# Moving one row of DRAM copies later, and summing half of an output projection in loaded tiles instead of with accumulating DMAs

## The chip, the cores and the metric

The kernel runs on one core of a Trainium2 chip. TensorE (PE) does the matmuls, VectorE (DVE) and ScalarE (ACT) do the elementwise work, GpSimd (POOL) issues the accumulating DMAs, and SyncE (SP) issues all other DMAs, in one in-order queue. The metric is the device time in microseconds of one execution; lower is better, and the median of several executions counts.

## The reference

A decoder trunk of one layer, 1024 tokens by 2048 channels, fp32:

```
hn = rmsnorm(h, norm_gain)
proj = hn @ w_in
pool_in, pool_gate, ssm_in, ssm_gate = four blocks of 1024 columns of proj
ya = pool_mixer(pool_in, w_pool, pool_scale) * silu(pool_gate)
yb = ssm_mixer(ssm_in, ...) * silu(ssm_gate)
h = h + concatenate([ya, yb]) @ w_out
h = h + (p @ w_ple) * sigmoid(h @ w_ple_gate)
return rmsnorm(h, final_gain)
```

## The kernel before, in words

Activations are kept transposed (channels on the 128 partitions, tokens along the row, 512 tokens to a half). Each fp32 operand is split in a rounded high part and a low rest, and a product is three matmuls (high by high, high by low, low by high). The split of a weight tile is a ScalarE cast (L204 in the output projection) and a VectorE subtraction (L103).

**Steps.** The program is one list of steps, written out in order by `emit(s)`. A step issues weight loads and the stores that have become due (`store(o, i, n)` is issued n+1 steps later, by SP), splits the weights of steps up to two ahead, calls the functions hung on it as `pre`, issues its matmuls, and calls those hung on it as `post`, which evacuate PSUM. So the position of a function in the step list sets where its instructions stand in each engine's in-order queue.

**Units.** The output projection is 8 units of 14 steps of 12 matmuls each: a unit makes 256 channels by two halves of 512 tokens of 512 columns of `w_out`, with a Strassen-like scheme of seven products (`PRODS`) by b = 0, 1. `units[0..3]` sum over the first 1024 rows of `w_out` (n = 0: slab `("y", 0)`, made of ya), `units[4..7]` over the second 1024 (n = 1, yb), each for the four column groups cg = 0 to 3; in this text they are units 0 to 7. A unit has eight results (4 row blocks of 128 channels by 2 halves of 512 tokens, 256 KB each).

**How a result leaves.** The sum lives in DRAM: `xT_d`, 2048 channels by 1024 tokens, holds the residual. In `o_post`, ScalarE copies four of a unit's products (each by b) from PSUM to an SBUF tile `ot` (L1294), VectorE adds the others to it, and POOL adds the tile to `xT_d` with an accumulating DMA (L1288). That is done for all 8 units. The gate is computed from this sum, and its results (for the first 1536 channels) are later accumulated by POOL to a second copy of it, `z_d`. Three plain copies by SP, DRAM to DRAM, of 512 rows (2 MB) each, fill `z_d`:

```
    for cg in range(3):

        steps[units[5 + cg][1] + 8]["pre"].append(lambda cg=cg: sp.dma_start(
            out=z_d[cg * HT:(cg + 1) * HT], in_=xT_d[cg * HT:(cg + 1) * HT]))
```

They stand at step 8 of units 5, 6 and 7.

**The slab of the gate.** Units 8 to 13 (gate, `w_ple_gate`) multiply with the slab of the finished h. While units 6 and 7 still run, the first half of that slab is made: `sums_load` (L378) reads rows of `xT_d` into `cq` at unit 6's steps 1, 5, 9 and 13, `sums_make` forms four sums of them 5 steps later, which go to `cm_d` by plain stores (L186, three steps later); `comb_load` (L397) reads the 28 tiles `cb` of the slab, from `xT_d` or `cm_d`, into a pool of 32 slots as they become free in unit 7, and `comb_split` (L402 on ScalarE) casts them, from step 4 of unit 7 on. ScalarE is in order: what is behind a cast whose load has not landed waits, the next weight cast (L204) too.

**The last columns' weights.** `wl_d` in DRAM is filled from the last 512 columns of `w_ple_gate` by 16 plain copies DRAM to DRAM of 256 KB (L1527), one every two steps from step `i_wl` on; it is read only at the end of the kernel. `vu` (L857) and `vb` (L869) are the loads of the state-space branch's small products (L882), `raw` (L194) those of `w_in`.

Of the kernel before, what the change touches and what calls it, by code (L numbers as in the profile page):

```python
# [12 lines left out]
ALU = mybir.AluOpType  # L13
# [5 lines left out]
HT = 512  # L19
# [20 lines left out]
def hybrid_trunk(ctx: ExitStack, tc: tile.TileContext, x, p, norm_gain, w_in, w_pool, pool_scale,  # L40
# [3 lines left out]
    sp = nc.sync  # L44
    dve = nc.vector
# [6 lines left out]
    out = out[0]  # L52
# [19 lines left out]
    xT_d = dr.tile([D, L], F32, name="xT_d")  # L72
# [11 lines left out]
    z_d = dr.tile([3 * HT, L], F32, name="z_d")  # L84
# [5 lines left out]
    def st(dt=F32, shape=(P, HT), name="st"):  # L90
        return st_p.tile(list(shape), dt, tag="st", name=name)
# [10 lines left out]
    def tt(eng, o, a, b, op):  # L102
        eng.tensor_tensor(out=o, in0=a, in1=b, op=op)  # L103
# [46 lines left out]
    steps = []  # L150
# [20 lines left out]
    banks = {}  # L171
# [5 lines left out]
    def store(o, i, n=1):  # L177

        late.append([n, o, i])
# [190 lines left out]
    def pair(src, i, h):  # L370
        return src[i * P:(i + 1) * P, h * HT:(h + 1) * HT]
# [159 lines left out]
    for h in range(2):  # L531
        for c0 in range(0, KD, 4):
# [7 lines left out]
            for kk, mb in chs:  # L540
                k = c0 + kk
                first.setdefault((h, k // 2), len(steps))
                last = k + 2 == KD
# [4 lines left out]
    for (h, j), at in first.items():  # L548
        at = max(1, at - X1)
# [5 lines left out]
    for h in range(2):  # L555
        at = first[h, 7] - 4
# [556 lines left out]
    def in_block(mb, halves=(0, 1)):  # L1113
        block(in_cols(mb), ALLK, halves, hn_key, ("pi", mb), v_post(mb))
        if 1 in halves:
            steps[-1]["post"].append(lambda: bg.append(pool_win(mb // 2, mb % 2)))
# [10 lines left out]
    in_block(6)  # L1127
    in_block(7)
    i_g = len(steps)
    i_wl = i_g - 120  # L1130
    in_block(4)
    pool_mm(3)
    in_block(5)
# [140 lines left out]
    for i in range(8):  # L1274
        at = i_g + 5 * i
# [7 lines left out]
    def o_post(n, cg):  # L1283
        def post(prod, b):
            name = ("o", n, cg)

            def add(c, h, t):
                pool.dma_start(out=pair(xT_d, 4 * cg + 2 * c + b, h), in_=t, accum_op=ALU.add)  # L1288

            if prod in ("11", "s2", "s3", "s4"):  # L1290
                k, c, h = {"11": ("a", 0, 0), "s2": ("a", 0, 1), "s3": ("e", 1, 1),
                           "s4": ("a", 1, 0)}[prod]
                t = ot[c, h, b] = st(name="ot")
                act.copy(out=t, in_=banks[name, k, b])  # L1294
                if prod == "s4":
                    add(c, h, ot.pop((c, h, b)))
                return
            k, c, h = {"12": ("f", 0, 0), "s1": ("a", 1, 1), "22": ("e", 0, 1)}[prod]
            t = ot.pop((c, h, b))
            tt(dve, t, banks[name, k, b], t, ALU.add)  # L1300
            add(c, h, t)
        return post

    units = []
# [8 lines left out]
    zt = {}  # L1313

    def z_load(src, mb, h, key):
        zt[key, mb, h] = st(name="z" + key)
        sp.dma_start(out=zt[key, mb, h], in_=pair(src, mb, h))
# [39 lines left out]
                                ps_d if key == "s" else e_d, mb, h, key))  # L1357
    for cg in range(3):

        steps[units[5 + cg][1] + 8]["pre"].append(lambda cg=cg: sp.dma_start(  # L1360
            out=z_d[cg * HT:(cg + 1) * HT], in_=xT_d[cg * HT:(cg + 1) * HT]))
    i_d = len(steps)
    for i, (u, s0) in enumerate(units):
        at = (units[i - 1] if i else gu[3])[1] + 2
# [6 lines left out]
    for j, s0, d in ((0, gu[1][1], 6), (1, i_c, 7), (3, units[6][1] - 3, 4), (4, units[8][1], 6)):  # L1371
        for kp in range(4):
            at = s0 + 4 + d * kp
# [3 lines left out]
    for j, s0 in ((0, gu[3][1]), (1, units[3][1]), (2, None), (3, units[7][1]),  # L1377
                  (4, units[10][1])):
        for i, prod in enumerate(PRODS):
            for kp in range(4):  # L1380
                n = 4 * i + kp
                if s0 is not None:
                    at = s0 + 2 * i + 4 + kp // 2
                elif n < 12:
                    at = i_last0 + 5 + n
                else:
                    at = i_last1 + 2 + (n - 12)
# [135 lines left out]
    for k in range(KD):  # L1523
        at = s_l + 4 + 2 * (k // 4) + k % 4 // 2
# [3 lines left out]
            out=wl_d[k * P:(k + 1) * P], in_=w_ple_gate[:, k, 3 * GW:]))  # L1528
    steps[s_l - 8]["pre"].append(fg_load)
    for tb in range(NB):  # L1530
        for g in range(4):
            at = s_l + 2 + g // 2 if tb == 0 else i_t[0] + g - 1 if tb == 1 else i_t[tb - 2] + g
            steps[at]["pre"].append(lambda tb=tb, g=g: h_load(tb, g))
            at = max(at + 3, i_t[tb - 1] + g) if tb else s_l + 6 + g
            steps[at]["pre"].append(lambda tb=tb, g=g: h_split(tb, g))
            if tb == 0:
                at = i_t[0] + {3: 1, 0: 2, 1: 3, 2: 4}[g]
            else:
                at = i_t[tb] + g + (tb == 1)
# [80 lines left out]
```

## Time and profile before

| what | value |
|---|---|
| median of 3 executions | 1695.04 us (1694.57 to 1695.71) |
| the profiled execution | 1694.17 us |
| its span | 1692.4 us |
| PE busy | 1650.8 us (98%) |
| DVE, ACT, POOL busy | 1116.8, 716.7, 160.2 us |
| DMA moved | 340.61 MB, mean 201 GB/s |

The span runs from the first to the last instruction that the profiler recorded; the device time of the same execution is 1.77 us longer. Busy shares are averages over the whole span. Where a change is made in one stage, the rows of that stage are to be read: its window, what ended TensorE's idle time there, and what the DMA engines did in it.

### The profile page before, as it was taken

Reading aid. Unit: us, or ns where it says so; the run is one execution under the profiler, and the core shown is the slowest. Engines: PE = TensorE matmul, PEld = TensorE weight load, DVE = VectorE, ACT = ScalarE, POOL = GpSimd, SP = SyncE. Lnnn points to the kernel's source line nnn. Section 1 sums busy time; section 2 is a strip of 40 time slices with the busy share of each in tenths; the row PEclk is TensorE's granted clock in tenths of the full one; section 3 lists DMA queues with packets and bytes.
Section 4 is the critical chain, followed back from the end, with each engine's and each line's share of the span. In section 5 each row is a group of like instructions: output and inputs, shape, how many; then the busy total and the mean of one; then the engine's idle time right before and its main releaser. Section 6 shows DMA issues by size and latency. Waiting matters only on the chain.

```text
span 1692.4 us, 22974 instructions
## 1 busy us (share of the span) xinstructions
PE 1650.8 (98%) x7622; PEld 1364.9 (81%) x7622; DVE 1116.8 (66%) x2148; ACT 716.7 (42%) x1511; POOL 160.2 (9%) x267
## 2 busy tenths in 40 slices
PE   8999999999999999999999999999999899999997
PEld 7888887887888888888778877888887688788886
DVE  6763699458797765555745778557646666877754
ACT  6652255352213552334643345335432533634553
POOL 0067000000000210000000000211111100011100
PEclk9999999999999999999999999999999899999999
DMA  8862444672233772687884576869679966989995
GB/s 264 253 189 74 117 133 138 197 207 89 75 113 100 217 213 73 186 233 227 275 300 149 189 271 205 225 156 274 147 183 267 318 232 225 340 221 264 273 281 158
DMA packets 334408, 340.61 MB, mean 201 GB/s; under 512 B 56281, under 2 KB 225266, under 8 KB 333298
## 3 DMA queue, kind: packets, MB, share of 16 engines
q1 hardware_dynamic: 321618, 316.07, 58.2%
q0 software_dynamic: 12672, 23.07, 8.6%
q8 instruction: 60, 0.98, 0.2%
q14 instruction: 58, 0.48, 0.1%
HBM read 226.34 MB, written 123.21 MB: 207 GB/s over the span
## 4 chain that ended last, share of the span: by engine, by line
PE 49%; DMA 4%; DVE 3%; issue 2%; ACT 1%; SPq 0%; ACTq 0%; POOLq 0%; POOL 0%; DVEq 0%
PE mm L236 24%; PE aux L236 10%; PE mm L258 8%; PE mm L248 5%; DMA cb<-cm_d 1%; DVE cb L103 1%; PE bk L1459 1%; DVE w L103 1%; DMA cb<-ya_d 1%; DMA wq<-in_w_ple_gate_dram 1%; DMA e_d<-et 1%; DMA cb<-xT_d 0%; DMA wl<-wl_d 0%; DVE zs L103 0%; DMA zs<-ps_d 0%
## 5 line engine op out<-in xcount | busy, mean ns | idle before, releaser
L258 PE MATMUL mm<-hn,w 128*128 128x512 f32 x3072 | 721.8, 392 | 1.7 <-DVE w L103 1.2
L258 PEld LDWEIGHTS mm<-hn,w 128*128 128x128 f32 x3072 | 571.7, 188 | 119.7 <-DVE w L103 1.6
L236 PE MATMUL mm<-cb,w 128*128 128x512 f32 x2160 | 500.9, 391 | 8.1 <-ACT w L204 3.2
L236 PEld LDWEIGHTS mm<-cb,w 128*128 128x128 f32 x2160 | 405.5, 188 | 97.9 <-DVE w L103 5.2
L214 ACT CAST w<-raw 128x256 fp32r<-128x256 f32 x324 | 128.1, 407 | 279.2 <-PE mm L258 224.7
L103 DVE TENSOR_TENSOR w<-raw,w 128x256 fp32r<-128x256 f32 (+1 forms) x328 | 141.3, 442 | 120.0 <-ACT w L214 111.8
L103 DVE TENSOR_TENSOR w<-wq,w 128x512 fp32r<-128x512 f32 x216 | 148.6, 688 | 104.0 <-ACT w L204 103.6
L236 PE MATMUL aux<-cb,w 128*128 128x512 f32 x864 | 205.9, 393 | 6.7 <-ACT w L204 6.5
L236 PEld LDWEIGHTS aux<-cb,w 128*128 128x128 f32 x864 | 163.3, 190 | 43.5 <-ACT w L204 8.3
L204 ACT CAST w<-wq 128x512 fp32r<-128x512 f32 x216 | 133.6, 620 | 138.5 <-PE mm L236 55.8
L1288 POOL DMA_DIRECT2D xT_d<-ot x64 | 55.4, 866 | 669.5 <-DVE ot L103 636.0
L103 DVE TENSOR_TENSOR cb<-cb 128x512 fp32r<-128x512 f32 x140 | 91.8, 687 | 32.8 <-ACT cb L402 26.5
L402 ACT CAST cb<-cb 128x512 fp32r<-128x512 f32 x140 | 82.1, 621 | 39.6 <-DMA cb<-xT_d 14.3
L248 PE MATMUL mm<-wl,h 128*128 128x512 f32 (+1 forms) x432 | 96.5, 374 | 0.0
L248 PEld LDWEIGHTS mm<-wl,h 128*128 128x128 f32 x432 | 72.9, 189 | 11.9
L103 POOL TENSOR_TENSOR ytm<-yt,mask 128x512 f32<-128x512 f32 x16 | 20.1, 1255 | 446.8 <-DMA yl<-L_d 316.6
L1294 ACT COPY ot<-mm 128x512 f32<-128x512 f32 x48 | 28.2, 588 | 75.7 <-PE mm L236 75.7
L892 DVE COPY V<-aux 64x128 f32<-64x128 f32 x64 | 24.5, 382 | 29.8 <-ACT V L894 29.6
L103 DVE TENSOR_TENSOR wq<-wq 128x1024 f32<-128x1024 f32 x36 | 43.9, 1219 | 0.0
L500 ACT ACTIVATE gs<-mm 128x512 f32<-128x512 f32 x32 | 18.9, 599 | 58.1 <-DVE mm L103 58.0
L1325 POOL DMA_DIRECT2D z_d<-zs x24 | 20.7, 863 | 216.1 <-DVE zs L103 216.1
L894 ACT COPY V<-aux 64x128 f32<-64x128 f32 x64 | 24.4, 381 | 31.1 <-DVE V L892 22.4
(213 smaller groups left out, 1557.3 us busy)
## 6 DMA issues: line engine op xcount, KB each, us to landing
raw<-in_w_in_dram SPq DMA_DIRECT2D x136, 256.0 KB, 3.0
cb<-cm_d SPq DMA_DIRECT2D x80, 256.0 KB, 5.2
wq<-in_w_out_dram SPq DMA_DIRECT2D x16, 1024.0 KB, 9.2
xT_d<-ot POOLq DMA_DIRECT2D x64, 256.0 KB, 6.5
cm_d<-cq SPq DMA_DIRECT2D x48, 256.0 KB, 4.1
wq<-in_w_ple_gate_dram SPq DMA_DIRECT2D x12, 1024.0 KB, 9.0
xT_d<-xt SPq DMA_DIRECT2D x32, 256.0 KB, 3.9
wq<-in_w_glu_dram SPq DMA_DIRECT2D x16, 512.0 KB, 7.3
```

The costliest lines, as they stand in the source:

```text
L103: eng.tensor_tensor(out=o, in0=a, in1=b, op=op)
L204: act.copy(out=w[0], in_=src)
L214: act.copy(out=w[:, 0], in_=raw)
L236: pe.matmul(out=banks[key], lhsT=w[wi][:, kp], rhs=a[:, ai], start=bool(new) and n == 0, stop=n == 11, skip_group_check=True)
L248: pe.matmul(out=banks[key][:, part], lhsT=a[:, ai, cols], rhs=b[:, part], start=start and j == 0, stop=stop and j == 2)
L258: pe.matmul(out=banks[key], lhsT=w[:, wi, i], rhs=a[:, ai], start=start and i == 0 and j == 0, stop=stop and i == 1 and j == 2)
L402: act.copy(out=sl[:, 0], in_=f(sl[:, 1]))
L892: dve.tensor_copy(out=o.rearrange("p k c -> p c k"), in_=i)
L894: act.copy(out=o.rearrange("p k c -> p c k"), in_=i)
L1288: pool.dma_start(out=pair(xT_d, 4 * cg + 2 * c + b, h), in_=t, accum_op=ALU.add)
L1294: act.copy(out=t, in_=banks[name, k, b])
L1325: pool.dma_start(out=pair(z_d, mb, h), in_=t, accum_op=ALU.add)
```

## The change

Two edits. First, `i_wl` is 28 steps later, and so all 16 copies to `wl_d`. Second, in the units of n = 1 with cg < 3 (units 4, 5 and 6), eight tiles `zs` are loaded from `xT_d` three steps ahead of their first use (24 loads by SP), VectorE adds every product to the loaded tile, and the finished tile is stored twice by SP, to `xT_d` and to `z_d` (48 stores). In those units the ScalarE copies and the accumulating DMAs are gone, and the three copies `z_d<-xT_d` too. Unit 7 (cg = 3) leaves as before.

```diff
-    i_wl = i_g - 120
+    i_wl = i_g - 92
...
             def add(c, h, t):
                 pool.dma_start(out=pair(xT_d, 4 * cg + 2 * c + b, h), in_=t, accum_op=ALU.add)
 
+            if n and cg < 3:
+                k, c, h, last = {
+                    "11": ("a", 0, 0, 0), "12": ("f", 0, 0, 1), "s2": ("a", 0, 1, 0),
+                    "s3": ("e", 1, 1, 0), "s1": ("a", 1, 1, 1), "s4": ("a", 1, 0, 1),
+                    "22": ("e", 0, 1, 1)}[prod]
+                mb = 4 * cg + 2 * c + b
+                t = zt["s", mb, h]
+                tt(dve, t, banks[name, k, b], t, ALU.add)
+                if last:
+                    del zt["s", mb, h]
+                    store(pair(xT_d, mb, h), t)
+                    store(pair(z_d, mb, h), t, 2)
+                return
...
     for cg in range(3):
 
-        steps[units[5 + cg][1] + 8]["pre"].append(lambda cg=cg: sp.dma_start(
-            out=z_d[cg * HT:(cg + 1) * HT], in_=xT_d[cg * HT:(cg + 1) * HT]))
+        for at, c, h in ((0, 0, 0), (4, 0, 1), (6, 1, 1), (10, 1, 0)):
+            for b in range(2):
+                steps[units[4 + cg][1] + at + b - 3]["pre"].append(
+                    lambda mb=4 * cg + 2 * c + b, h=h: z_load(xT_d, mb, h, "s"))
```

**SP at the state-space products, before.** Weight copies stand between the loads of `raw`, `vb` and `vu`:

```order
L1527 DMA wl_d_94<-in_w_ple_gate_dram 128x512
L194 DMA raw_3377<-in_w_in_dram 128x4x128
L1527 DMA wl_d_94<-in_w_ple_gate_dram 128x512
L869 DMA vb_3385<-B_d_97 128x512
L857 DMA vu_3386<-u_d_84 128x4x128
L869 DMA vb_3404<-B_d_97 128x512
L857 DMA vu_3405<-u_d_84 128x4x128
L194 DMA raw_3420<-in_w_in_dram 128x4x128
L1527 DMA wl_d_94<-in_w_ple_gate_dram 128x512
```

Of the nine rows three are weight copies, one of them straight ahead of the first `vb`. **The same place after the change:**

```order
L194 DMA raw_3371<-in_w_in_dram 128x4x128
L869 DMA vb_3378<-B_d_97 128x512
L857 DMA vu_3379<-u_d_84 128x4x128
L869 DMA vb_3397<-B_d_97 128x512
L857 DMA vu_3398<-u_d_84 128x4x128
L194 DMA raw_3413<-in_w_in_dram 128x4x128
```

The weight copies are gone from there. **The place where they stand now**, behind the last `vu`, in the stretch in which the scan runs:

```order
L857 DMA vu_3839<-u_d_84 128x4x128
L869 DMA vb_3870<-B_d_97 128x512
L857 DMA vu_3871<-u_d_84 128x4x128
L194 DMA raw_3899<-in_w_in_dram 128x4x128
L1542 DMA wl_d_94<-in_w_ple_gate_dram 128x512
L194 DMA raw_3958<-in_w_in_dram 128x4x128
L1542 DMA wl_d_94<-in_w_ple_gate_dram 128x512
```

They alternate with the loads of `raw`, with no `vu` behind them.

**SP at the end of unit 6, before.** `cq` is read once the `cm_d` stores ahead of it are issued; `wq` is unit 8's weights:

```order
L378 DMA cq<-xT_d 128x512 x4
L186 DMA cm_d<-cs 128x512
L186 DMA cm_d<-cq 128x512 x3
L378 DMA cq<-xT_d 128x512 x4
L330 DMA wq<-in_w_ple_gate_dram 128x4x512 x2
L397 DMA cb<-xT_d 128x512 x2
```

No store of a result stands here, since POOL issues those. **The same place after:**

```order
L186 DMA cm_d<-cq 128x512 x3
L186 DMA z_d<-zs 128x512
L186 DMA xT_d<-zs 128x512
L378 DMA cq<-xT_d 128x512 x4
L186 DMA z_d<-zs 128x512
L186 DMA xT_d<-zs 128x512
L186 DMA z_d<-zs 128x512
L186 DMA xT_d<-zs 128x512
L186 DMA z_d<-zs 128x512
L330 DMA wq<-in_w_ple_gate_dram 128x4x512 x2
L397 DMA cb<-xT_d 128x512 x2
```

The results of unit 6 are stored here now, each to `xT_d` and to `z_d`: five of these stores came between the last `cq` loads and `wq`.

**SP in unit 7, before**, from the slab's loads to the next `wq`:

```order
L397 DMA cb<-xT_d 128x512 x6
L397 DMA cb<-cm_d 128x512 x2
L186 DMA cm_d<-cs 128x512
L186 DMA cm_d<-cq 128x512 x3
L397 DMA cb<-cm_d 128x512 x2
L1360 DMA z_d<-xT_d 32x16384
L397 DMA cb<-cm_d 128x512 x12
L397 DMA cb<-xT_d 128x512 x4
L330 DMA wq<-in_w_ple_gate_dram 128x4x512 x2
```

The copy to `z_d` stands ahead of twelve of the slab's loads. **After:**

```order
L397 DMA cb<-xT_d 128x512 x6
L397 DMA cb<-cm_d 128x512 x2
L186 DMA cm_d<-cs 128x512
L186 DMA cm_d<-cq 128x512 x3
L397 DMA cb<-cm_d 128x512 x14
L397 DMA cb<-xT_d 128x512 x4
L330 DMA wq<-in_w_ple_gate_dram 128x4x512 x2
```

The copy is gone, and nothing stands in its place.

## Rows read from the trace of the kernel before

**Rows 1.** The page: busy time of the engines over the span.

```profile
PE 1650.8 (98%) x7622; PEld 1364.9 (81%) x7622; DVE 1116.8 (66%) x2148; ACT 716.7 (42%) x1511; POOL 160.2 (9%) x267
```

**Rows 2.** Windows over units 3 to 7, then a stretch inside unit 7.

```profile
core 0: us, PE busy (x) PEld busy (x) DVE busy (x) ACT busy (x) POOL busy (x), PEclk, DMA share, GB/s
1143.35:1181.43 38.08, 38.08 (x169) 31.54 (x168) 29.38 (x44) 23.01 (x43) 6.90 (x8) 1.00 0.97 273
1181.43:1219.51 38.08, 38.08 (x169) 31.54 (x168) 22.57 (x33) 16.65 (x31) 6.91 (x8) 1.00 0.59 139
1219.51:1257.59 38.08, 38.08 (x169) 31.54 (x168) 17.83 (x24) 12.58 (x23) 6.90 (x8) 1.00 0.72 166
1257.59:1295.67 38.08, 38.08 (x169) 31.54 (x168) 23.01 (x32) 12.60 (x23) 6.90 (x8) 1.00 0.93 254
1295.67:1348.92 53.25, 43.81 (x169) 33.95 (x168) 34.13 (x51) 23.03 (x43) 6.44 (x8) 0.90 0.99 316
1344.00:1348.00 4.00, 4.00 (x10) 3.12 (x11) 3.85 (x7) 4.00 (x9) 1.75 (x2) 0.50 1.06 382
```

**Rows 3.** Timeline of TensorE, unit 7: start, length, form, idle before.

```profile
1305.67 8.04 PE L236 MATMUL mm<-cb,w 128*128 128x512 f32 x34 [1.22 <-DVE w L103]
...
1322.52 0.73 PE L236 MATMUL mm<-cb,w 128*128 128x512 f32 x2 [2.72 <-ACT w L204]
...
1343.73 5.36 PE L236 MATMUL aux<-cb,w 128*128 128x512 f32 x12 [4.69 <-ACT w L204]
```

**Rows 4.** Timeline of ScalarE, unit 7.

```profile
1313.65 0.62 ACT L402 CAST cb<-cb 128x512 fp32r<-128x512 f32 x1 [4.90 <-DMA cb<-xT_d]
...
1340.18 0.62 ACT L402 CAST cb<-cb 128x512 fp32r<-128x512 f32 x1 [8.28 <-DMA cb<-cm_d]
```

**Rows 5.** Timeline of SP's DMA issues, units 6 and 7.

```profile
1274.22 0.51 SPq L1360 DMA_DIRECT2D z_d<-xT_d  x1
...
1301.21 1.75 SPq L378 DMA_DIRECT2D cq<-xT_d  x4
...
1328.66 0.47 SPq L1360 DMA_DIRECT2D z_d<-xT_d  x1
1329.24 14.45 SPq L397 DMA_DIRECT2D cb<-cm_d  x12
...
1346.75 1.01 SPq L330 DMA_DIRECT2D wq<-in_w_ple_gate_dram  x2
```

**Rows 6.** Waits of SP's DMA issues, 1290 to 1350: total, times, longest.

```profile
SPq L397 <- DMA z_d<-xT_d: 5.0, 1, 5.0
```

**Rows 7.** DMA issues in unit 7's window: KB each, median us to landing.

```profile
cm_d<-cq SPq DMA_DIRECT2D x6, 256.0 KB, 9.2
```

**Rows 8.** The whole span's DMA queues and two kinds of issue.

```profile
q1 hardware_dynamic: 321618, 316.07, 58.2%
q0 software_dynamic: 12672, 23.07, 8.6%
...
ps_d<-zs SPq DMA_DIRECT2D x24, 256.0 KB, 3.8
...
z_d<-xT_d SPq DMA_DIRECT2D x3, 9.3
```

**Rows 9.** ScalarE's and VectorE's evacuations, units 4 to 6.

```profile
L1294 ACT COPY ot<-mm 128x512 f32<-128x512 f32 x18 | 10.6, 589 | 33.0 <-PE mm L236 33.0
L103 DVE TENSOR_TENSOR ot<-mm,ot 128x512 f32<-128x512 f32 x12 | 8.3, 690 | 11.6 <-PE mm L236 11.6
```

**Rows 10.** Waits of TensorE over the whole span, one of its lines.

```profile
PE aux L882 <- DMA vu<-u_d: 4.9, 3, 2.3
```

**Rows 11.** Timeline of SP's DMA issues around 345 us.

```profile
343.97 0.50 SPq L1527 DMA_DIRECT2D wl_d<-in_w_ple_gate_dram  x1
...
347.06 0.37 SPq L857 DMA_DIRECT2D vu<-u_d  x1
```

**Rows 12.** Window over the scan's stretch.

```profile
388.00:476.00 88.00, 88.00 (x390) 72.83 (x389) 71.77 (x222) 18.70 (x45) 0.00 (x0) 1.00 0.28 84
```

## The prediction

> **What bounds the kernel now.** I read the busy times first: TensorE works 1650.8 of 1692.4 us [rows 1]. So nothing that other engines or the DMAs do counts unless TensorE waits for it, and all idle time together is 41.6 us. The change takes no matmul away. The question is therefore which of those 41.6 us end on something that it moves.
>
> The windows by unit answer that for the second edit [rows 2]. Units 3 to 6 each take 38.08 us, with TensorE busy throughout and at its full granted clock (1.00, the 2.4 GHz level). Unit 7 has the same 169 matmuls and takes 53.25 us: 15.17 us more. Of these, 53.25 - 43.81 = 9.44 us are idle, and 43.81 - 38.08 = 5.73 us are matmuls at a lower clock: it is 0.90 over the unit, and 0.50 (the 1.2 GHz level) in the window that begins 0.3 us after the longest wait ended. What idled TensorE in unit 7 is in its timeline: 1.22 us on a VectorE weight tile, 2.72 and 4.69 us on ScalarE's weight casts [rows 3]. ScalarE itself, in order, was held ahead of those casts by slab casts whose loads had not landed: 4.90 us at 1313.65, 8.28 us before 1340.18 [rows 4]. The loads were late because the DMA engines were full: their share is 0.99 in unit 7 and 1.06 in its last stretch, against 0.59 to 0.93 in units 4 to 6 [rows 2]. Into this stretch SP issues, at 1328.66, the last of the 2 MB copies to z_d, and right behind it twelve slab loads that take 14.45 us to issue [rows 5]; one slab load's issue waited 5.0 us for that kind of copy alone, which it does not read [rows 6].
>
> For the first edit, the state-space products waited 4.9 us in three waits for vu [rows 10].
>
> **Prices.** The accumulating queue took 8.6% of the span, 145.5 us of all 16 engines, for 23.07 MB, which is 88 DMAs of 256 KB: 1.65 us each. The plain queue took 58.2%, 985 us, for 316.07 MB or 1206 times 256 KB: 0.82 us each [rows 8]. A 2 MB copy at that rate is 8 x 0.82 = 6.5 us; it lands 9.3 us after its issue [rows 8].
>
> **Units 4 to 6.** Per unit the second edit removes eight accumulates (13.2 us) and one copy (6.5): 19.7 us of DMA work. It adds eight loads and sixteen stores: 24 x 0.82 = 19.7 us. The work is equal; its place is not. Unit 4 goes from 0.59 x 38.08 = 22.5 us to 29.0, since no copy fell into it; unit 5 stays at 27.4 and unit 6 near 35.4 [rows 2]. All three stay under 38.08, so I cost this at nothing, hidden by TensorE's 38 us. VectorE gets eight more adds of 0.69 us, 5.5 us a unit, on top of 18 to 23 busy us of 38; ScalarE loses eight copies of 0.589, 4.7 us [rows 2, 9]. GpSimd's issues end with the accumulates.
>
> The new wait here is VectorE's first add for its zs load. Behind it in VectorE's queue stand the weight subtractions, for which TensorE would wait. The loads are issued three steps ahead, 3 x 2.72 = 8.2 us, and weights are split up to two steps ahead, another 5.4 us. A load would have to land more than 13.6 us after its issue before TensorE feels it; the slowest group in full unit 7 took a median of 9.2 us [rows 7]. I take nothing, and keep the loss for a rival.
>
> **Unit 7.** DMA work before: 0.99 x 53.25 = 52.7 us. What changes:
> - the copy at 1328.66: -6.5;
> - the four cq loads of 1301.21 [rows 5]. They belong to unit 6's last step, and were late by the copy of 1274.22, which delayed the stores ahead of them. With the copy gone they go back to unit 6: 4 x 0.82 = -3.3;
> - one accumulate of unit 6 that was issued at its end: -1.7;
> - five stores of unit 6's last results, which become due as unit 7 begins: +4.1;
> - the next weights that SP issued at 1346.75 [rows 5], which no step of unit 7 needs: -2.0 of their 6.5 by the unit's end.
>
> That makes 43.3 us of work to do in the 38.08 us, 5.2 too much. Of this the last two accumulates of unit 7 (3.3) can land in unit 8, since nothing reads them in unit 7. It leaves 1.9, and I leave the 1.22 us wait for VectorE too, because it ends on weight sums that the change doesn't touch: together 3.1 us of 15.2 stay, most of the slow clock goes with the waits, and about 12.2 us are gained. The bounds: at least the copy's own 6.5 us, if all the rest of the list is wrong; at most the whole 15.2.
>
> How would it be by unit 3? It holds 0.97 x 38.08 = 36.9 us of DMA work without any wait [rows 2]. So a unit can run with the DMA engines nearly full, and 43.3 less 3.3 is just beyond. That is why I take a value near the upper end.
>
> **First edit.** One copy is 0.50 us of SP's issue and 0.82 us of DMA work, 1.3 us. The vu load of 347.06 was issued 3.1 us behind such a copy [rows 11]; the three waits add up to 4.9 us, the longest 2.3 [rows 10]. If each shrinks by one copy's 1.3, 3.9 us go. Bounds: nothing, if vu waits for its own landing; 4.9, if all goes. In the new place, 388 to 476 us, TensorE is busy all 88 us and the DMA share is 0.28 [rows 12]: 16 copies of 0.82 us are 13 us beside 63 free ones. I cost the new place at nothing. Their reader is at the end of the kernel.
>
> **Sum.** 1694.17 - 12.2 - 3.9 = 1678.1 for the profiled execution. The median of the runs is 0.87 above it, so I predict **1679.0 us**, its own range 1675 (15.2 and 4.9 gained) to 1684.
>
> **Rivals.**
> *Unit 7 stays bound by DMA, because many small DMAs cost more than their bytes.* For it: with DMA shares near 1 the median cm_d store took 9.2 us to land [rows 7], and SP keeps eight lanes in flight, by the listing of the program; 9.2 / 8 = 1.15 us each. Then the 24 DMAs of a unit cost 27.6 us instead of 19.7. Units 4 and 5 still fit; unit 6 has 35.4 + 7.9 = 43.3, and 5.2 us run over into unit 7, which then has 48.5, a loss of 10.4 of the 15.2. With the first edit: 1695.04 - 4.8 - 3.9 = 1686, between 1684 and 1690. Against it: the plain queue's 0.82 is a mean that is made of just such DMAs, and ps_d stores of that size land in 3.8 us in a quieter stretch [rows 8].
> The Trainium skill speaks for this rival ("DMA: Bandwidth & Descriptors", section "Measured (HBM→SBUF, 128 partitions, SWDGE, issued from GpSimd)"): it asks for transfers of 1 MiB and more, and has 0.95 us for 64 KB and 6.15 for 1 MB. Between these in a straight line, an estimate from that page, 256 KB take 1.99 us, 0.45 more than a quarter of 1 MB; eight stores in place of a copy would cost 3.6 us more, and the sum would be about 1682. No row here shows both sizes side by side, and the sum above does not use it.
>
> *The copy was not what held unit 7.* The slab's loads need slots that come free only as products retire; if that sets their time, the second edit gives nothing, and with half of the first the time is 1693, within 0.2% (about 3.4 us, what this kernel's measurement can tell from no change). Against it: the DMA share of 0.99 over the whole unit, which free engines would not show. The same time comes out if new stalls in units 4 to 6 eat the gain.
>
> *Slower: VectorE stalls on late zs loads.* SP is in order too, and a store that waits for a late add holds the loads behind it. The point from which it decides is the 13.6 us above: each further microsecond of landing counts at four places (pairs of loads) in three units, 12 us. A landing of 15.2 us costs 19 us and brings the time past 1698; 15.5 gives about 1702. Unit 6, with 0.93, is where it would start. Against it: nothing in unit 7, at 0.99, took that long in the median.
>
> **Chances.** Forecast 0.62; unit 7 still bound 0.24; within 0.2% 0.06; slower 0.07; still faster than 1674.5 0.01. So faster 0.87, same 0.06, slower 0.07. The range is 1674.5 to 1689: above it lie the 0.13 of the last cases and a little of the second.
>
> **What would show it.** Right: unit 7's window near 41 us, its clock near 1.00, no wait of TensorE over 2 us in it; units 4 to 6 at 38.08 with DMA shares of 0.75, 0.72 and 0.93; cq's last loads issued before 1296; vu waits under 2 us together; the scan's stretch still 88 us busy. Wrong: unit 7 with ScalarE's casts still waiting several microseconds for cb (first rival), any idle TensorE in units 4 to 6 that ends on VectorE (last rival), or waits in the scan's stretch for raw, which would mean that the copies cost there what they gave back.

## The result, and the profile after

The changed kernel takes 1680.78 us in the median of 4 runs (1679.13 to 1682.31), the kernel before beside it 1694.8 us. The ratio is 0.9917, with a 95% interval of 0.9903 to 0.9931: 14 us faster, and the time lies 1.8 us above the predicted 1679.0, inside the likeliest case's own range. The profiled execution took 1679.31 us with a span of 1677.5, 14.9 us less than before.

The page of the changed kernel, busy time and the two big queues, to be read beside [rows 1, 8]:

```profile
PE 1646.2 (98%) x7622; PEld 1363.1 (81%) x7622; DVE 1129.3 (67%) x2172; ACT 705.6 (42%) x1487; POOL 139.5 (8%) x243
...
q1 hardware_dynamic: 331842, 328.66, 60.5%
q0 software_dynamic: 9216, 16.78, 6.2%
```

The number of matmuls is the same. The accumulating queue lost 6.3 MB (24 DMAs), the plain queue gained 12.6 MB.

The windows over units 4 to 7 of the changed kernel, columns as in [rows 2]:

```profile
1175.12:1213.20 38.08, 38.08 (x169) 31.53 (x168) 27.22 (x41) 12.69 (x23) 0.86 (x1) 1.00 0.69 224
1213.20:1251.28 38.08, 38.08 (x169) 31.53 (x168) 22.61 (x32) 8.71 (x15) 0.00 (x0) 1.00 0.61 221
1251.28:1289.36 38.08, 38.08 (x169) 31.53 (x168) 27.69 (x40) 8.72 (x15) 0.00 (x0) 1.00 0.89 324
1289.36:1334.48 45.12, 40.37 (x170) 32.10 (x168) 34.60 (x52) 23.00 (x43) 6.04 (x7) 0.96 0.96 312
```

Units 4 to 6 are still without a wait, at 38.08 us. Unit 7 fell from 53.25 to 45.12 us, its clock from 0.90 only to 0.96. The DMA share of unit 5, which had held a copy, fell from 0.72 to 0.61.

TensorE's timeline there shows what is left, beside [rows 3]:

```profile
1289.36 8.78 PE L236 MATMUL mm<-cb,w 128*128 128x512 f32 x38
1299.36 8.04 PE L236 MATMUL mm<-cb,w 128*128 128x512 f32 x34 [1.23 <-DVE w L103]
...
1315.99 1.05 PE L236 MATMUL mm<-cb,w 128*128 128x512 f32 x2 [3.12 <-ACT w L204]
1317.45 11.75 PE L236 MATMUL mm<-cb,w 128*128 128x512 f32 x46 [0.41 <-DVE w L103]
1329.04 5.60 PE L236 MATMUL aux<-cb,w 128*128 128x512 f32 x24
1334.48 16.48 PE L236 MATMUL mm<-cb,w 128*128 128x512 f32 x72
```

The late wait of 4.69 us is gone: the matmuls follow each other from 1317.45 us on. The early ones stayed: 1.23 us on VectorE, and 3.12 where before it was 2.72 on ScalarE. ScalarE's casts that held it, beside [rows 4]:

```profile
1307.15 1.27 ACT L402 CAST cb<-cb 128x512 fp32r<-128x512 f32 x2 [4.41 <-DMA cb<-xT_d]
...
1313.64 1.30 ACT L402 CAST cb<-cb 128x512 fp32r<-128x512 f32 x2 [4.21 <-DMA cb<-xT_d]
```

They waited for slab tiles from xT_d. SP issued those so, beside [rows 5]:

```profile
1289.17 2.74 SPq L378 DMA_DIRECT2D cq<-xT_d  x4
...
1295.48 1.54 SPq L330 DMA_DIRECT2D wq<-in_w_ple_gate_dram  x2
1297.12 1.65 SPq L397 DMA_DIRECT2D cb<-xT_d  x2
...
1303.15 7.42 SPq L397 DMA_DIRECT2D cb<-xT_d  x6
...
1316.34 10.23 SPq L397 DMA_DIRECT2D cb<-cm_d  x14
```

In the kernel before, SP's issue of the same group of six was this row:

```profile
1310.38 9.75 SPq L397 DMA_DIRECT2D cb<-xT_d  x6
```

The last cq loads went at 1289.17, 0.2 us ahead of unit 7's start (1289.36); before, they went 5.5 us behind it (1301.21 against 1295.67). But the slab's first loads hardly came sooner: the group of six at 1303.15 is 13.8 us behind the unit's start, against 14.7 before. Between cq and those six stand five stores of results, unit 8's weights, two other slab loads, and the stores of the sums.

For the first edit, the two ends of the state-space stretch, the wait ahead of it and the last product. Changed kernel:

```profile
269.19 0.66 PE L753 MATMUL aux<-ident,m 128*128 128x128 f32 x4 [1.28 <-DVE m L103]
...
382.47 1.05 PE L882 MATMUL aux<-vu,vb 128*128 128x128 f32 x8
```

Kernel before:

```profile
268.24 0.66 PE L753 MATMUL aux<-ident,m 128*128 128x128 f32 x4 [1.31 <-DVE m L103]
...
386.91 1.05 PE L882 MATMUL aux<-vu,vb 128*128 128x128 f32 x8
```

From 268.24 to 386.91 are 118.67 us, from 269.19 to 382.47 are 113.28: 5.39 us less, and no wait for vu is left.

Where the 14.9 us of the spans are: 0.95 lost ahead of the stretch (269.19 against 268.24), 5.39 gained in it, 1.87 gained from its end to unit 7's start (908.76 against 906.89 us), 8.13 in unit 7, 0.46 behind it. The 1.87 lie in code that neither edit touches: some 1.3 around one wait near 860 us (3.85 us in the profile of before, 3.42 in that of after) and in the 77 us of matmuls behind it, and 0.6 in a wait near 1006 us.

### The profile page after: what moved, and what is told of

The parts are those of the page before. It is cut to its first block, busy times and chain, and to the rows that moved or that the text cites. A ratio compares the mean times of both kernels' runs of the same rounds, so it can differ in the third digit from the quotient of the medians.

```text
span 1677.5 us, 22990 instructions
## 1 busy us (share of the span) xinstructions
PE 1646.2 (98%) x7622; PEld 1363.1 (81%) x7622; DVE 1129.3 (67%) x2172; ACT 705.6 (42%) x1487; POOL 139.5 (8%) x243
## 3 DMA queue, kind: packets, MB, share of 16 engines
q1 hardware_dynamic: 331842, 328.66, 60.5%
## 4 chain that ended last, share of the span: by engine, by line
PE 50%; DMA 3%; DVE 3%; issue 2%; ACT 1%; SPq 0%; ACTq 0%; POOLq 0%; POOL 0%; DVEq 0%
PE mm L236 25%; PE aux L236 10%; PE mm L258 9%; PE mm L248 5%; DVE cb L103 1%; PE bk L1474 1%; DMA wq<-in_w_ple_gate_dram 1%; DMA cb<-ya_d 1%; DMA zs<-ps_d 1%; DMA cb<-xT_d 0%; DVE w L103 0%; DMA wl<-wl_d 0%; ACT cb L402 0%; DMA e_d<-et 0%; DVE pf L103 0%
## 5 line engine op out<-in xcount | busy, mean ns | idle before, releaser
L1288 POOL DMA_DIRECT2D xT_d<-ot x40 | 34.7, 868 | 679.9 <-DVE ot L103 665.1
L103 DVE TENSOR_TENSOR zs<-mm,zs 128x512 f32<-128x512 f32 x72 | 49.6, 688 | 30.8 <-PE mm L236 30.6
L1307 ACT COPY ot<-mm 128x512 f32<-128x512 f32 x30 | 17.7, 588 | 44.5 <-PE mm L236 44.5
```

## The experiments

My theory: the copies to z_d held unit 7, by where their DMA work stood, and the copies to wl_d held the vu loads; that results leave by stores instead of accumulates is worth little by itself. The rival: the dear accumulates held unit 7, and loaded sums are what frees it.

In the table, "unit 7" runs from its first matmul to that of unit 8. "Six loads" is how long behind the unit's start SP came to the group of six slab loads from xT_d. "Early" is the wait for ScalarE (in one kernel VectorE) in the middle of the unit, "late" the one near its end. "Stretch" is as above, 268 to 387 us. Waits under 0.3 us are left out. These columns are from one profile of each kernel; the ratios are from all its runs.

| kernel | ratio to before (95%) | stretch | unit 7 | six loads | early, late |
|---|---|---|---|---|---|
| before | 1 | 118.67 | 53.25 | 14.7 | 2.72, 4.69 |
| the change | 0.9917 (0.9903 to 0.9931) | 113.28 | 45.12 | 13.8 | 3.12, none |
| first edit alone | 0.9966 (0.9951 to 0.9981) | 112.97 | 55.38 | 15.8 | 3.27, 6.28 |
| second edit alone | 0.9926 (0.9907 to 0.9944) | 116.96 | 42.27 | 12.3 | 0.89, none |
| copies late | 0.9905 (0.9885 to 0.9924) | 120.64 | 40.34 | 11.2 | none, none |
| unit-7 copy late | 0.9952 (0.9936 to 0.9968) | 119.48 | 46.14 | 14.7 | 3.12, none |
| unit-6 copy late | 0.9951 (0.9934 to 0.9968) | 118.06 | 48.39 | 11.9 | 0.52, 4.84 |
| change, copies kept | 0.9949 (0.9934 to 0.9963) | 113.67 | 50.77 | 14.2 | 2.85, 2.42 |
| change, copies late | 0.9893 (0.9878 to 0.9909) | 113.64 | 39.64 | 9.5 | none, none |
| change, last by copy | 0.9901 (0.9883 to 0.9918) | 113.81 | 39.60 | 10.1 | none, none |
| change, weights late | 0.9906 (0.9887 to 0.9925) | 113.47 | 44.70 | 11.4 | 3.22, none |
| both moves | 0.9900 (0.9885 to 0.9916) | 113.62 | 41.91 | 11.6 | 0.46, none |
| small copies | 0.9979 (0.9968 to 0.9989) | 113.10 | 53.06 | 15.1 | 1.73 and 1.41, 5.06 |
| copies by GpSimd | 1.0043 (1.0027 to 1.0058) | 112.99 | 57.00 | 16.4 | 3.80, 7.76 |

**First edit alone** (kernel before, copies to wl_d later).

```diff
-    i_wl = i_g - 120
+    i_wl = i_g - 92
```

> The kernel before with the first edit alone (the copies to wl_d begin 28 steps later). My theory: a copy ahead of vu's loads delays them in SP's queue and in the DMA engines; all three waits for vu (4.9 us) go, the units 4 to 7 stay as before (unit 7 near 53 us), and the time falls by 4 to 6 us. Rival: the vu loads' own landing sets the waits and the whole gain of the change comes from the second edit; then the waits for vu stay near 4.9 us and the time falls by less than 1 us.

Measured: 1689.91 us, 5.8 below before; the stretch falls by 5.7 us, and no wait for vu is left. Unit 7 keeps its two waits, as TensorE's timeline of this kernel shows:

```profile
1291.80 8.78 PE L236 MATMUL mm<-cb,w 128*128 128x512 f32 x38
...
1341.93 5.41 PE L236 MATMUL aux<-cb,w 128*128 128x512 f32 x12 [6.28 <-ACT w L204]
1347.18 13.11 PE L236 MATMUL mm<-cb,w 128*128 128x512 f32 x57
```

So the first edit is worth 5 to 6 us by itself and does not help unit 7.

**Second edit alone** (the change with i_wl as before).

```diff
-    i_wl = i_g - 92
+    i_wl = i_g - 120
```

> The change without its first edit (copies to wl_d where they were before; sums in loaded tiles, two stores). My theory: unit 7 takes 45 us as in the change, the waits for vu stay at 4.9 us, and the time falls by 8 to 10 us. Rival (first edit has no effect of its own): the time falls by the whole 14 to 15 us.

Measured: 1684.15 us, 11.5 below before; unit 7 takes 42.27 us, less than in the change itself, whose unit 7 has the same instructions. So with the same instructions unit 7 differs by 2.85 us between two profiles, and smaller differences in the table count for little. This profile is of an execution of 1680.05 us, 4.1 below its kernel's median, so it may flatter the kernel. The stretch stays at 117 us: it waited 1.5 us for vu and 2.0 us for VectorE's copies behind an earlier vu.

**Copies late** (kernel before; only the three copies to z_d move, to units 8, 9 and 10; the accumulates stay).

```diff
-        steps[units[5 + cg][1] + 8]["pre"].append(lambda cg=cg: sp.dma_start(
+        steps[units[8 + cg][1] + 8]["pre"].append(lambda cg=cg: sp.dma_start(
```

> The kernel before with its three 2 MB copies to z_d three units later (units 8, 9, 10 instead of 5, 6, 7); accumulates as before. My theory (the copies' DMA work in units 6 and 7 was what held unit 7): the 4.7 us wait in unit 7 goes, unit 7 takes 44 to 47 us, and the time falls by 6 to 9 us, less what units 8 to 10 lose to the copies. Rival (the accumulates, dear and in the way of SP's loads, held it): unit 7 stays at 51 us or more and the time falls by less than 3 us.

Measured: 1680.01 us, 15.7 below before. That is as far as the whole change gets (the intervals overlap), with one line. TensorE in unit 7:

```profile
1294.89 8.77 PE L236 MATMUL mm<-cb,w 128*128 128x512 f32 x38
1304.89 8.03 PE L236 MATMUL mm<-cb,w 128*128 128x512 f32 x34 [1.22 <-DVE w L103]
...
1324.23 5.72 PE L236 MATMUL mm<-cb,w 128*128 128x512 f32 x24 [0.22 <-ACT cb L402]
1329.79 5.60 PE L236 MATMUL aux<-cb,w 128*128 128x512 f32 x24
1335.23 16.48 PE L236 MATMUL mm<-cb,w 128*128 128x512 f32 x72
```

Of the waits for ScalarE 0.22 us are left, and the unit takes 40.34 us. Units 8 to 10, which now hold the copies, lost nothing: each takes 38.08 us with TensorE busy throughout. SP's issues into it:

```profile
1293.72 1.82 SPq L378 DMA_DIRECT2D cq<-xT_d  x4
...
1299.17 1.55 SPq L397 DMA_DIRECT2D cb<-xT_d  x2
...
1306.08 7.24 SPq L397 DMA_DIRECT2D cb<-xT_d  x6
```

The cq loads go 1.2 us ahead of the unit, the six slab loads 11.2 behind its start. The rival falls with this as the main cause: with all accumulates in place unit 7 is no slower than in the change.

**Unit-7 copy late, unit-6 copy late** (kernel before; of the copies only the third moves, to unit 10, or only the second, to unit 9).

```diff
-        steps[units[5 + cg][1] + 8]["pre"].append(lambda cg=cg: sp.dma_start(
+        steps[units[(5, 6, 10)[cg]][1] + 8]["pre"].append(lambda cg=cg: sp.dma_start(
...
+        steps[units[(5, 9, 7)[cg]][1] + 8]["pre"].append(lambda cg=cg: sp.dma_start(
```

> The kernel before with only the last of the three copies to z_d moved (from unit 7 to unit 10); that in unit 6 stays. By the terms of the prediction the unit-7 copy is worth 6.5 us of DMA work there and the unit-6 copy another 3.3 through the late cq loads: unit 7 at 43 to 46 us, the time 5 to 9 us below that of before, between before and all copies late. Rival (the copy in unit 6 alone held it, by making cq and the sums late): unit 7 stays above 50 us.

> The kernel before with only the second of the three copies to z_d moved (from unit 6 to unit 9); that in unit 7 stays. If the two copies make two separate waits (the one in unit 6 the early wait for slab tiles from xT_d, the one in unit 7 the late wait for tiles from cm_d), the early wait falls under 1 us, the late wait of 4 to 6 us stays, unit 7 takes 46 to 49 us and the time falls by 4 to 7 us. Rival (all DMA work of unit 7 counts as one sum over the unit, whatever its place): only the four cq loads leave it, 3.3 us, unit 7 takes 49 to 51 us.

Measured: unit 7 at 46.14 and 48.39 us. With the unit-7 copy away TensorE's timeline has the early wait and no late one:

```profile
1323.06 0.73 PE L236 MATMUL mm<-cb,w 128*128 128x512 f32 x2 [3.12 <-ACT w L204]
...
1336.70 5.60 PE L236 MATMUL aux<-cb,w 128*128 128x512 f32 x24
1342.14 16.48 PE L236 MATMUL mm<-cb,w 128*128 128x512 f32 x72
```

With the unit-6 copy away it has the late one, and little of the early:

```profile
1318.21 0.74 PE L236 MATMUL mm<-cb,w 128*128 128x512 f32 x2 [0.52 <-ACT w L204]
...
1338.47 4.35 PE L236 MATMUL aux<-cb,w 128*128 128x512 f32 x12 [4.84 <-ACT w L204]
1342.65 16.57 PE L236 MATMUL mm<-cb,w 128*128 128x512 f32 x72
```

Each copy makes one of the two waits. Against 53.25 us they are worth 7.1 and 4.9 us, together 12.0; all three copies moved give 12.9. In time the two moves brought 8.5 and 8.3 us (the second more than I expected), all three together 15.7.

The rival of the second of these runs, one sum of DMA work over the unit, gave 49 to 51 us for it. The measured 48.39 lies 0.6 us below that, which is less than unit 7 differs between profiles of the same instructions; so the pattern of the waits speaks for two separate waits, but the length does not refute the sum.

How each copy made its wait can be read in part from what SP waited for, from 1285 to 1350 us. In the kernel before, the cq loads waited for the stores of the sums to land:

```profile
SPq L378 <- DMA cm_d<-cq: 16.0, 2, 8.6
```

With the unit-6 copy late, this fell, and SP's own wait for the unit-7 copy stayed, as in [rows 6]:

```profile
SPq L397 <- DMA z_d<-xT_d: 5.5, 1, 5.5
SPq L378 <- DMA cm_d<-cq: 4.5, 2, 2.6
```

With the unit-7 copy late instead, the cq loads waited 15.7 us, as before. So the unit-6 copy delayed the stores that the cq loads wait for. The unit-7 copy had two ways to delay the slab loads behind it: its DMA work, and the 5 us for which SP, in order, waited for the copy before it issued one of them. No run separates these two.

**Change, copies kept** (the change without the second store, the three copies back in units 5 to 7).

```diff
-                    store(pair(z_d, mb, h), t, 2)
...
+        steps[units[5 + cg][1] + 8]["pre"].append(lambda cg=cg: sp.dma_start(
+            out=z_d[cg * HT:(cg + 1) * HT], in_=xT_d[cg * HT:(cg + 1) * HT]))
```

> The change with the second store (to z_d) taken out and the three 2 MB copies put back where they stood (units 5, 6, 7); the sums stay in loaded tiles, the first edit stays. My theory (the copies in units 6 and 7 held unit 7): unit 7 goes back above 50 us, with a wait of 4 us or more for ScalarE late in it, and the time is near that of the first edit alone, 1688 to 1692 us. Rival (the accumulates in units 4 to 6 held it): unit 7 stays at 42 to 46 us, the time near 1681 us.

Measured: 1687.46 us, 9.2 below before, of which the first edit has 5.8; unit 7 takes 50.77 us, with the early wait and a late one again:

```profile
1318.27 1.22 PE L236 MATMUL mm<-cb,w 128*128 128x512 f32 x2 [2.85 <-ACT w L204]
...
1338.09 4.82 PE L236 MATMUL aux<-cb,w 128*128 128x512 f32 x12 [2.42 <-ACT w L204]
```

So without 24 of the accumulates, but with the copies, unit 7 takes 2.3 to 4.6 us less than in the kernels that keep both in SP's order (53.06 to 55.38 us), and the time falls by 3.4 us more than with the first edit alone. The intervals of these two ratios overlap, and the 2.3 us are within what unit 7 differs by between profiles: the copies have the large share, and a small one of the accumulates is possible but not shown.

**Change, copies late** (the kernel of the last run, with the copies in units 8 to 10).

```diff
-        steps[units[5 + cg][1] + 8]["pre"].append(lambda cg=cg: sp.dma_start(
+        steps[units[8 + cg][1] + 8]["pre"].append(lambda cg=cg: sp.dma_start(
```

> The change with the second store taken out and the three copies in units 8, 9 and 10 instead. My theory: unit 7 takes 40 to 43 us, since only three stores of unit 6 fall into it instead of five; time 1676 to 1680 us. Rival (loaded sums cost unit 7 something whatever fills z_d): unit 7 stays at 45 us, 1681 us.

Measured: 1677.98 us, the lowest ratio of all, 0.9893; unit 7 takes 39.64 us. It and the kernel with both moves, below, differ only in how the results of units 4 to 6 leave (loaded sums and one store, or copies from PSUM and accumulates): 0.9893 and 0.9900, intervals that overlap.

**Change, last by copy** (the change, but unit 6's rows of z_d by one copy in unit 10).

```diff
-                    store(pair(z_d, mb, h), t, 2)
+                    if cg < 2:
+                        store(pair(z_d, mb, h), t, 2)
...
+    steps[units[10][1] + 8]["pre"].append(lambda: sp.dma_start(
+        out=z_d[2 * HT:], in_=xT_d[2 * HT:3 * HT]))
```

> The change, but the z_d rows of unit 6 are filled by one 2 MB copy in unit 10 instead of eight stores; units 4 and 5 store twice as in the change. If the five stores of unit 6's results that fall into unit 7 are what is left of its loss (4.1 us of DMA work by the prediction's list), only three are left, unit 7 takes 40 to 42 us and the time is 2 to 4 us below the change's. Rival (the loss left varies by itself, or comes from units 4 and 5's many small DMAs): unit 7 at 43 to 46 us.

Measured: 1677.79 us, ratio 0.9901. SP's six slab loads and TensorE's rows around what was the early wait:

```profile
1302.62 6.21 SPq L397 DMA_DIRECT2D cb<-xT_d  x6
```

```profile
1302.51 8.00 PE L236 MATMUL mm<-cb,w 128*128 128x512 f32 x34 [1.23 <-DVE w L103]
...
1315.79 11.04 PE L236 MATMUL mm<-cb,w 128*128 128x512 f32 x48
...
1332.11 16.48 PE L236 MATMUL mm<-cb,w 128*128 128x512 f32 x72
```

Two stores of unit 6's results stand between the last cq loads and unit 8's weights, where the change has five (I had expected three). SP comes to the loads 10.1 us behind the unit's start instead of 13.8, no early wait for ScalarE is left, and the unit takes 39.60 us. That is also 2.7 us less than the 42.27 of the second edit alone, the better of the two profiles with five stores and the same order. Units 4 and 5 keep all their small stores here and have half of them in the run above (39.64 us), so these cost unit 7 nothing. Against the change it is 3.0 us in the medians, with intervals of the ratios that overlap.

**Change, weights late** (the change; unit 8's weights are loaded at step 6 of unit 7).

```diff
-        at = (units[i - 1] if i else gu[3])[1] + 2
+        at = (units[i - 1] if i else gu[3])[1] + (6 if i == 8 else 2)
```

> The change with one more edit: unit 8's 2 MB of weights are loaded at step 6 of unit 7 instead of step 2, behind the first slab loads instead of ahead of them. My theory: what is left in unit 7 (a wait of 3.1 us for ScalarE, held by casts of slab tiles read from xT_d) is the slab's first loads queued behind these weights; the wait falls under 1 us, unit 7 takes 40 to 42 us, and the time falls by 17 to 20 us against before. Rival (the loads wait for slots, or for the stores ahead of them): unit 7 stays near 45 us, the time as with the change.

Measured: 1680.79 us, as the change. The early wait moved rather than went, as TensorE's row and then ScalarE's show:

```profile
1325.73 7.32 PE L236 MATMUL mm<-cb,w 128*128 128x512 f32 x24 [3.22 <-DVE ot L103]
```

```profile
1323.04 1.20 ACT L402 CAST cb<-cb 128x512 fp32r<-128x512 f32 x2 [4.47 <-DMA cb<-cm_d]
```

The six loads came sooner (11.4 us behind the start) and the wait for ScalarE is gone. But TensorE waits 3.22 us a step later, for VectorE, which in its own queue stood behind these casts, and they waited 4.47 us for the next slab loads, those from cm_d. The weights now stand ahead of these instead of the first. My theory of this run missed in the unit's length and in the time: 2 MB moved from ahead of one group of needed loads to ahead of the next moved the wait along with it.

**Both moves** (kernel before with the first edit and the three late copies; accumulates kept).

```diff
-    i_wl = i_g - 120
+    i_wl = i_g - 92
...
-        steps[units[5 + cg][1] + 8]["pre"].append(lambda cg=cg: sp.dma_start(
+        steps[units[8 + cg][1] + 8]["pre"].append(lambda cg=cg: sp.dma_start(
```

> The kernel before with two moves and nothing else: the copies to wl_d 28 steps later, the copies to z_d three units later; the accumulates stay. My theory: the gains of the two add up (about 5 and 15): 1674 to 1678 us, faster than the change, with unit 7 at 40 to 41 us. Rival (what the first edit gives is run-to-run difference): as with the late copies alone, 1680 us.

Measured: 1678.52 us, ratio 0.9900, against 0.9905 with the late copies alone. The stretch falls from 120.64 to 113.62 us, as expected, but the intervals do not show it in the time: in this profile the wait ahead of the stretch stood at 270.75 us instead of 267.89, and unit 7 took 41.91 us instead of 40.34. This is inconclusive on whether the two gains add up in full.

**Small copies** (kernel before; 16 of each copy's 128 rows where it stood, 112 rows 28 steps later).

```diff
-            out=wl_d[k * P:(k + 1) * P], in_=w_ple_gate[:, k, 3 * GW:]))
+            out=wl_d[k * P:k * P + 16], in_=w_ple_gate[0:16, k, 3 * GW:]))
+        steps[i_wl + 28 + 2 * k]["pre"].append(lambda k=k: sp.dma_start(
+            out=wl_d[k * P + 16:(k + 1) * P], in_=w_ple_gate[16:P, k, 3 * GW:]))
```

> The kernel before with each of the 16 copies to wl_d cut in two: the first 16 of its 128 rows are copied where the whole copy stood, the other 112 rows 28 steps later. So SP issues just as many copies beside the vu loads, with an eighth of their DMA work. If SP's issue and the lanes' order make vu late, the waits for vu (and VectorE's for the products behind them) stay at 3 to 5 us and the stretch from the wait at 268 us to the last of these products stays near 118 us. If the DMA work does, the stretch falls to 113 or 114 us as with the first edit.

Measured: ratio 0.9979. The ends of the stretch in TensorE's timeline:

```profile
269.24 0.66 PE L753 MATMUL aux<-ident,m 128*128 128x128 f32 x4 [1.31 <-DVE m L103]
...
382.34 1.05 PE L882 MATMUL aux<-vu,vb 128*128 128x128 f32 x8
```

The stretch is 113.10 us, as short as with the first edit, with as many copies issued by SP beside the vu loads, at 0.5 us each as before. So it was their DMA work, not the issue. The time falls by 3.2 us, less than the 5.8 of the first edit alone; the intervals of the two overlap.

**Copies by GpSimd** (kernel before; the same copies issued by GpSimd's queue).

```diff
-        steps[i_wl + 2 * k]["pre"].append(lambda k=k: sp.dma_start(
+        steps[i_wl + 2 * k]["pre"].append(lambda k=k: pool.dma_start(
```

> The kernel before with the 16 copies to wl_d issued by GpSimd's queue instead of SP's, at the same steps: the same DMA work, but not in SP's order. If SP's order is what makes the vu loads late (a copy's issue and its place among eight lanes), the waits for vu fall under 1.5 us in all and the time falls by 3 to 6 us. If it is the DMA work beside them, the waits stay at 3.5 to 5 us and the time is within 1.5 us of before.

Measured: 1702.61 us, 5.9 above before. It tells nothing on its question: GpSimd has nothing to wait for there, and issued all 16 from 161.4 to 173.4 us. The loads of the state-space constants then came late; TensorE's waits have a row that the kernel before lacks:

```profile
PE aux L784 <- DMA cn<-in_c_im_dram: 7.7, 1, 7.7
```

The stretch is 112.99 us long, since the copies were over by then.

## Why the prediction was right, and where its terms were off

**Right:** that the change is faster, by 14 us where 16 were forecast; that unit 7 and the vu waits are the two places; that units 4 to 6 hide all 72 new DMAs and the additional adds; that cq's last loads go back to unit 6 (1289.17, before the 1296 that I gave); that the late wait went with the copy; that the new place of the wl_d copies costs nothing (TensorE is busy all 88 us from 388 to 476 us, with the DMA share at 0.43 instead of 0.28 [rows 12]).

Part of the closeness is luck. The two terms of the sum, 16.1 us, came to 13.5; of the 14.9 us between the two spans, 1.4 came from stretches that the sum left out and neither edit touches.

**Unit 7: 12.2 forecast, 8.13 measured.** The list of DMA work was right in size. The change's window has a DMA share of 0.96 over 45.12 us, which is 43.3 us of work, the sum of the list. The step that failed is the one from this work to the time, "It leaves 1.9", and with the VectorE wait 3.1 us. Measured, the unit lost 7.04 us: 1.23 and 0.41 waiting for VectorE, 3.12 for ScalarE, and 2.29 in matmuls at a lower clock (40.37 us busy instead of 38.08). The early wait for ScalarE, 2.72 us before, which I had let go with the rest, stayed. The work was taken as one amount, without asking what stands ahead of the loads that ScalarE needs first. The five stores of unit 6's results stood in the list as +4.1 us; in the trace they stand ahead of the slab's first loads, which came 13.8 us behind the unit's start, where the copy in unit 6 had kept them at 14.7. With two of these stores instead of five the wait is gone, in two profiles (39.60 and 39.64 us). The list priced the copy in unit 6 at 3.3 us, the work of four cq loads; moved alone it is worth 4.9 us in the unit, no further from the price than two profiles can differ.

How far the total of DMA work binds as well stays open. The windows over unit 7 of three more kernels (the second edit alone, the weights late, the copies late; columns as in [rows 2]):

```profile
1292.95:1335.22 42.27, 39.20 (x169) 31.24 (x168) 34.39 (x52) 22.99 (x43) 6.04 (x7) 1.00 1.02 327
1293.62:1338.32 44.70, 40.26 (x169) 32.55 (x168) 32.80 (x49) 22.86 (x42) 5.18 (x6) 0.96 0.98 315
1294.89:1335.23 40.34, 38.89 (x169) 31.33 (x168) 33.89 (x51) 23.28 (x43) 6.92 (x8) 1.00 1.02 314
```

The share times the length is 43.1, 43.8 and 41.1 us of work. In all the profiles of these kernels unit 7's share lies between 0.96 and 1.02, so its length goes with the work in it, from 40.0 us of work in 39.64 us (the change with its copies late) to 55.3 in 57.00 (the copies by GpSimd). A longer unit also takes in more of the work that follows, so this does not say which sets which. But the work alone does not fix the time: 43.1 to 43.8 us of it took 42.27 us in one kernel, 44.70 and 45.12 in two others.

**First edit: 3.9 forecast, 5.4 measured in the stretch** (5.3 on the mean of five profiles with the copies in their old place, 118.8 us, and seven with all of them in the new, 113.5). I took one copy's SP issue and DMA work for each wait; with the copies gone the three waits go, but for 0.2 to 0.6 us in some of the profiles. Of the two parts of my price, the small copies show that the DMA work is the whole of it.

**The equal work of units 4 to 6** (19.7 us out, 19.7 in) was too cautious: unit 5's share went from 0.72 to 0.61, so there 24 plain DMAs cost about 4.2 us less than eight accumulates and the copy. By the page, the plain queue's time grew by 60.5% of 1677.5 less 58.2% of 1692.4, 30 us, for 72 DMAs more and three copies less; with the copies at the 6.5 us each of my estimate, that is about 0.69 us a DMA. The first rival, which needed 1.15, falls with this, though part of its result (unit 7 still held) came true for another reason. The rule of the Trainium skill that speaks for it ("DMA: Bandwidth & Descriptors", section "Measured (HBM→SBUF, 128 partitions, SWDGE, issued from GpSimd)"), to make transfers of 1 MiB and more, stands there beside loads issued from GpSimd; for SP's stores here it would have made the small stores dearer than the copy. The trace does not agree: with many of them in flight a DMA of 256 KB came to these 0.69 us, less than the 0.82 at which an eighth of a 2 MB copy was priced.

**The slower rival** did not come about: no wait in units 4 to 6. The rival that the copy was not what held unit 7 is refuted by the late copies: with them and nothing else moved, the unit takes 40.34 us.

**Open:** the early wait of unit 7 differs between two kernels with the same instructions there (0.89 in the second edit alone, 3.12 in the change). Whether the unit-7 copy held the slab loads by its work or by SP's wait for it is not separated. And the profiles with the wl_d copies late reach the stretch 269.2 to 271.0 us after the start, those with the copies in the old place 267.9 to 269.1, though the program is the same up to there. So of the 5.3 us that the stretch gains, about 1.5 are lost ahead of it on the mean of these profiles. The copies can't be the cause directly: they are first issued at 287 us, and the two groups of profiles already differ by 1.4 us at a wait near 78 us (77.7 against 79.1 on the mean). Why is not known.

## What to carry to other kernels

A large copy that nobody waits for can still be what an in-order engine waits for: ask which small load stands behind it, and whether the copy can go where no one is in a hurry; here that one line gave as much as a new way of storing the results. When costing a stage that is full of DMAs, don't stop at the sum of its work; list what is queued ahead of the first load that is needed, since stores put there can take the place of the copy that was taken away. Before an operation is replaced because it is dear, move it alone.

## What the runs showed of the hardware

An accumulating DMA of 256 KB took 6.2% of 1677.5 us over 64 of them, 1.6 us of all engines, twice a plain one's, as before [rows 8]; still, to remove 24 of them while the copies stayed brought no more than 3.4 us, which is within the intervals. With a DMA share of 1.02 unit 7 ran within 2.3 us of its undisturbed 38.08 (the copies late), which I had not expected. And a queue that waits for nothing issues at once: GpSimd's copies went out 126 us before the place (287 us) at which SP issues the first of them.
